# Attention's splits and products with v run on over the ends of head pairs, one unit later, with four tiles of transposed halves

## The chip, the cores and the metric

The kernel runs on one core of a Trainium2 chip. The metric is device time in microseconds (us) of that core for one launch. Before the change the median of three runs is 1622.26 us (1620.82 to 1622.88). The profiled execution was a run of its own, of 1619.84 us.

## The reference, cut to what matters

Two sequences, A and B, of 1024 tokens by 1024 channels go through the same two layers. Weights and inputs are float32. The even layer holds the attention:

```python
def even_layer(x, ...):
    h = rms_norm(x, norm_g)
    pu, pz, q, k, v, az = jnp.split(h @ w_in, EVEN_SPLITS, axis=-1)
    a_out = pool_mixer(pu, pool_w, pool_scale) * silu(pz)
    b_out = axial_gqa(q, k, v, ...) * silu(az)          # 8 query heads of 64, 2 key heads
    return x + concat([a_out, b_out], -1) @ w_out
# in axial_gqa, for each head:
    s = einsum('bqkgd,bskd->bkgqs', q, k) * scale       # 1024 x 1024 scores
    p = softmax(s, axis=-1)
    o = einsum('bkgqs,bskd->bqkgd', p, v)
def odd_layer(x, ...):
    u, vv, z = jnp.split(rms_norm(x) @ w_in, 3, axis=-1)
    sv = w_s (128 x 128 mixing per chunk) applied to rms_norm(gelu(vv)) + b_s
    return x + (gelu(u) * sv * silu(z)) @ w_out
```

## The kernel before, in words

Every float32 operand is cut into two float16 halves (a high part and the rest), and a product is three passes over them. TensorE (PE) does the products, ScalarE (ACT) and VectorE (DVE) cut, scale and take softmax, SyncE (SP) issues all DMAs, the transposing ones among them. Almost all tiles lie in one large SBUF tile, the arena, whose places a planner gives out from the order in which tiles are taken and freed in the Python code.

Attention of one sequence is four head pairs (`attention`, j = 0 to 3). A head pair is 16 units in four groups g: a unit is one tile of 128 queries of one of two heads, and a group is two tiles of two heads. In the texts units are numbered through, S0 to S63 for sequence A and S64 to S127 for B, and a group is written A2.1 (sequence, head pair, group). For a unit, `scores` writes 128 x 1024 scores into one of two PSUM tiles `ps_s` by 4 matmuls (L678), DVE takes the row maximum (L684), ACT the scaled maximum and exp (L685, L686). `split` (ACT L693, DVE L695, ACT L697, DVE L698) normalises and cuts the row into halves, and a transposing DMA (L699) puts them into a tile of the ring `pt`, which has three tiles, one for each group and head. `pv` multiplies a group by v with 48 matmuls (L710), the first half's weights in turn with the second's, one head each, so the first matmul reads head 0's tile and the second head 1's; DVE takes the result out (L714).

In the code, the split of a unit stands after the next unit's scores. The product of group g - 1 stands after the third unit of group g. At the end of a head pair the chain is brought to its end: last split, one portion of filler, last product, then the largest value of the output tile (DVE, L252) and its DMA to DRAM (L734).

Between units, `fill(rate)` puts in other work ("fillers"): the projections of the next head pairs, the pool branch, the other sequence's norms, and for A's rows the output projection (`out_chunks`) while B's attention runs. After A's attention all fillers are drained, `mix_back` brings seven tiles of A's mixed rows back from DRAM (L658), and `split_chunks` cuts the eight tiles into halves (DVE L753 and L756, ACT L755) with a scale over all eight, before the output projection can start.

The order on each engine is not that of the code: a scheduler reorders all instructions by its own model of their times, and each engine then runs its list strictly in that order.

Of the kernel before, what the change touches and what calls it, by code (L numbers as in the profile page):

```python
# [20 lines left out]
P = 128  # L21
# [178 lines left out]
class Kernel:  # L200
    def __init__(self, ctx, tc, args, order, plan):
        self.nc, self.tc, self.order = tc.nc, tc, order
        self.__dict__.update(args)
        self.one = one = ctx.enter_context(tc.tile_pool(name="one", bufs=1))
        self.kept = one.tile([P, 640], F32, name="kept")
        self.kept_at = 0
        self.rings, self.role = {}, "misc"
        self.blocks = {}
        self.arena = Arena(tc.nc, one, plan)
        self.get, self.free = self.arena.get, self.arena.free  # L210
        self.diff = one.tile([P, 2, L], F32R, name="diff")
        self.pw = one.tile([P, 2, 4, P], F32R, name="pw")
        self.ps_s = ctx.enter_context(tc.tile_pool(name="ps_s", bufs=2, space=PSUM))
        self.ps_g = ctx.enter_context(tc.tile_pool(name="ps_g", bufs=3, space=PSUM))
        self.ps_o = ctx.enter_context(tc.tile_pool(name="ps_o", bufs=1, space=PSUM))
        dram = ctx.enter_context(tc.tile_pool(name="dram", bufs=1, space=bass.MemoryType.DRAM))
        self.x1 = [dram.tile([L, D], F32, name=f"x1_{s}") for s in range(2)]
        self.mixed = [dram.tile([8, P, L], F32, name=f"mixed_{s}") for s in range(2)]
        self.w = {"in_e": self.w_in_e, "out_e": self.w_out_e, "in_o": self.w_in_o, "out_o": self.w_out_o}
        self.fillers = deque()  # L220
        self.credit = 0
        self.turned = {}


# [183 lines left out]
    def consts_even(self):  # L408
# [32 lines left out]
        nc.sync.dma_start(out=self.pscale, in_=self.pool_scale.rearrange("(g p) -> p g", p=P))  # L441
        self.edge = self.tiny([P, 4, 2, 8], keep="edge")
        nc.sync.dma_start(out=self.edge, in_=self.edges)
        self.pt = Ring(self, 3, [P, 2, NT, 256], F16)
        self.pf = Ring(self, 3, [P, L], F32)
        self.phl = Ring(self, 4, [P, 2, L], F16)

# [212 lines left out]
    def attention(self, st, j, rate):  # L660
# [28 lines left out]
        def split(tt, h, p, ss):  # L689
            if tt % 2 == 0:  # L690
                pts[tt // 2, h] = self.pt.get()
            s2 = self.tiny([P, 1])
            nc.scalar.activation(out=s2, in_=ss, func=AF.Copy, scale=2.0 ** -15)  # L693
            r = self.tiny([P, 1])
            nc.vector.reciprocal(out=r, in_=s2)  # L695
            hl = self.phl.get()
            nc.scalar.activation(out=hl[:, 0, :], in_=p, func=AF.Copy, scale=r[:, 0:1])  # L697
            nc.vector.scalar_tensor_tensor(out=hl[:, 1, :], in0=p, scalar=r[:, 0:1], in1=hl[:, 0, :], op0=ALU.mult, op1=ALU.subtract)  # L698
            nc.sync.dma_start_transpose(  # L699
                out=pts[tt // 2, h].rearrange("p a t n -> p (a t) n")[:, :, (tt % 2) * P:(tt % 2 + 1) * P],  # L700
                in_=hl.rearrange("p a n -> p (a n)"))
# [11 lines left out]
            cols = slice(g * 256, g * 256 + 256)  # L713
            nc.vector.scalar_tensor_tensor(out=out[:, cols], in0=ps, scalar=sc[:, 0:1], in1=sz[:, cols], op0=ALU.mult, op1=ALU.mult)  # L714

        prev = None
        for g in range(NT // 2):
            for h in range(2):
                for tt in (2 * g, 2 * g + 1):
                    with self.as_role("attention"):  # L720
                        cur = (tt, h) + scores(tt, h)
                        if prev:
                            split(*prev)
                    prev = cur
                    self.fill(rate)
                    if g and h == 1 and tt % 2 == 0:
                        pv(g - 1)
        with self.as_role("attention"):
            split(*prev)
        self.fill(rate)  # L730
        pv(NT // 2 - 1)
        self.amax(st.mam[:, 4 + j:5 + j], out)
        if j < 3:
            nc.sync.dma_start(out=self.mixed[st.s][4 + j], in_=out)  # L734
            self.free(out)
        else:
            st.mix[7] = out
        self.free(sz, st.qT.pop(j))

    def split_chunks(self, tiles, am, keep):  # L740

# [170 lines left out]
    def run(self):  # L912
# [6 lines left out]
        def spread(a, b):  # L919

            out, k = [], 0
            for i, c in enumerate(a):
                out.append(c)
                while k < len(b) and (k + 1) * len(a) <= (i + 1) * len(b):
                    out.append(b[k])
                    k += 1
            return out + b[k:]
# [4 lines left out]
        def pool(st, j):  # L932
            return self.pool_chunks(st, j)
# [31 lines left out]
        for j in range(4):  # L965
            self.attention(A, j, 2950)
        self.drain()
        self.mix_back(A)
        self.free(self.gain_e[0])
        parts_A, split_A = self.split_chunks(A.mix, A.mam, "mixA")  # L970
        self.free(A.kT, A.v)

        def odd_start():
            self.gain_o, self.dh_o = self.gain(self.norm_o, "go", 9)
# [1 line left out]
        nA = self.norm_chunks(A, hA2, self.x1[0], go_, False)  # L976
        vvA = self.vv_chunks(A, True)
        self.fillers.extend(
            spread(qa(B, 1), split_A) + pool(B, 0) + self.out_chunks("out_e", (parts_A, self.xs[0], self.x1[0])) + qa(B, 2) + pool(B, 1)
            + qa(B, 3) + let_go(lambda: [self.rope["q"]]) + [(0, odd_start)] + pool(B, 2) + spread(pool(B, 3), nA[:3]) + let_go(lambda: hB)  # L980
            + spread(vvA[:2], nA[3:]) + vvA[2:11])
        for j in range(4):
            self.attention(B, j, 4250)
        self.drain()
        self.mix_back(B)
        for ring in (self.pt, self.pf, self.phl):
# [100 lines left out]
```

## Time and profile before

| | |
|---|---|
| median of three runs | 1622.26 us |
| profiled execution, its own time | 1619.84 us |
| its span, first to last instruction | 1618.1 us |
| PE busy | 1496.5 us (92%) |
| DVE busy | 1061.8 us (66%) |
| ACT busy | 729.0 us (45%) |
| mean granted TensorE clock | 0.976 |

Attention lies between 78 and about 894 us of the span; A's units to 427 us, B's after it. In that part the matmuls of scores, products and fillers are mixed on PE. A row of the timeline names the engine, the line, what is written and read, and how many instructions are merged, and in brackets how long the engine stood idle before and who released it.

### The profile page before, as it was taken

The page shows a single profiled execution, that of the slowest core. Times are in us where ns is not written, and L with a number is a line of the kernel's source. Part 1 is how long each engine was busy: PE and PEld are TensorE (multiplying, and loading weights), DVE is VectorE, ACT ScalarE, POOL GpSimd, SP SyncE. Part 2 cuts the span into 40 slices and gives each one's busy share as a digit, 9 for nine tenths or more (in the row PEclk, how much of TensorE's full clock was granted, in tenths as well). Part 3 has the DMA queues.
Part 4 walks back from the last instruction along what each step waited for, and adds up shares of the span by engine and source line. Part 5 has one row for each costly group of instructions (what it writes and reads, how often), then busy time and mean ns, then how long its engine had stood idle before and what let it go on. Part 6 is the DMA issues. An engine that isn't in the chain of part 4 may idle for free.

```text
span 1618.1 us, 28061 instructions
## 1 busy us (share of the span) xinstructions
PE 1496.5 (92%) x11751; PEld 1014.1 (63%) x11751; DVE 1061.8 (66%) x1613; ACT 729.0 (45%) x1121; POOL 117.3 (7%) x187
## 2 busy tenths in 40 slices
PE   2989998878799999999799999999999999998999
PEld 1754654557456787464478887554488554467888
DVE  7899999889897675788975854466650643345211
ACT  4367767767664364566755811133432521111000
POOL 2410000102000000000200100010000200000000
PEclk9999999889889999999899999999999999999999
DMA  9558688899948877675997643157210023114121
GB/s 252 116 118 161 150 148 183 186 210 194 213 87 213 211 156 151 144 154 133 224 260 164 186 125 98 40 157 167 81 40 1 27 66 117 46 66 137 60 85 53
DMA packets 497152, 217.69 MB, mean 135 GB/s; under 512 B 366337, under 2 KB 488705, under 8 KB 497025
## 3 DMA queue, kind: packets, MB, share of 16 engines
q1 hardware_dynamic: 497024, 215.90, 57.0%
q8 instruction: 92, 1.51, 0.4%
q14 instruction: 36, 0.29, 0.1%
HBM read 101.04 MB, written 24.12 MB: 77 GB/s over the span
## 4 chain that ended last, share of the span: by engine, by line
PE 57%; DVE 16%; DMA 11%; issue 4%; ACT 4%; POOL 1%; SPq 1%; DVEq 0%; ACTq 0%; POOLq 0%
PE bank L399 35%; PE ps_s L399 17%; DMA arena<-arena 4%; PE bank L710 3%; DVE arena L698 3%; DVE ring_attention L684 3%; PE ps_s L678 3%; DMA arena<-in_w_in_e 2%; DMA arena<-in_w_in_o 1%; DMA arena<-x 1%; ACT arena L686 1%; DVE ring_weights L252 1%; DVE arena L170 1%; DVE arena L756 1%; DVE arena L622 1%
## 5 line engine op out<-in xcount | busy, mean ns | idle before, releaser
L399 PEld LDWEIGHTS <-arena 128*128 128x128 f16 x9600 | 863.9, 99 | 434.1 <-DMA arena<-arena 25.6
L399 PE MATMUL bank<-arena 128*128 128x256 f16 (+2 forms) x8064 | 941.1, 277 | 31.8 <-ACT arena L169 12.7
L399 PE MATMUL ps_s<-arena 128*128 128x512 f16 x1536 | 338.1, 380 | 2.4 <-DVE arena L170 2.4
L169 ACT ACTIVATE arena<-arena,kept 128x1024 f16<-128x1024 f32 x108 | 121.4, 1142 | 281.1 <-DVE kept L281 126.2
L170 DVE SCALAR_TENSOR_TENSOR arena<-arena,kept 128x1024 f16<-128x1024 f32 x108 | 137.6, 1288 | 80.9 <-ACT arena L169 63.9
L698 DVE SCALAR_TENSOR_TENSOR arena<-arena,ring_attention 128x1024 f16<-128x1024 f32 x128 | 163.2, 1278 | 31.3 <-ACT arena L697 29.9
L684 DVE TENSOR_REDUCE ring_attention<-ps_s 128x1 f32<-128x1024 f32 x128 | 155.0, 1216 | 10.8 <-PE ps_s L678 10.5
L697 ACT ACTIVATE arena<-arena,ring_attention 128x1024 f16<-128x1024 f32 x128 | 145.5, 1141 | 36.0 <-DVE ring_attention L695 27.1
L678 PE MATMUL ps_s<-arena 128*128 128x512 f16 x512 | 136.8, 394 | 26.2 <-ACT arena L686 21.5
L686 ACT ACTIVATE arena<-ps_s,ring_attention,kept 128x1024 f32<-128x1024 f32 x128 | 153.7, 1201 | 8.4 <-DVE ring_attention L695 3.7
L784 DVE SCALAR_TENSOR_TENSOR arena<-bank,ring_dout,arena 128x512 f32<-128x512 f32 x64 | 47.9, 749 | 149.7 <-PE bank L399 149.7
L710 PE MATMUL bank<-arena 128*64 128x256 f16 x1536 | 107.7, 290 | 35.7 <-DMA arena<-arena 34.3
L710 PEld LDWEIGHTS <-arena 128*64 128x64 f16 x1536 | 90.2, 117 | 61.2 <-DMA arena<-arena 31.6
L252 DVE TENSOR_REDUCE ring_weights<-arena 128x1 f32<-128x1024 f32 x58 | 70.2, 1215 | 66.6 <-DMA arena<-in_w_in_o 29.4
L678 PEld LDWEIGHTS <-arena 128*128 128x128 f16 x512 | 47.9, 100 | 81.1 <-issue 38.6
L685 ACT ACTIVATE ring_attention<-ring_attention,kept 128x1 f32<-128x1 f32 x128 | 37.1, 290 | 131.4 <-DVE ring_attention L684 131.0
L364 DVE SCALAR_TENSOR_TENSOR arena<-arena,ring_norm 128x1024 f32<-128x1024 f32 x32 | 41.8, 1306 | 25.7 <-POOL ring_norm L318 22.7
L362 ACT ACTIVATE arena<-arena 128x1024 f32<-128x1024 f32 x32 | 33.7, 1054 | 53.1 <-DMA arena<-x 32.9
L903 DVE TENSOR_TENSOR arena<-arena 128x1024 f32<-128x1024 f32 x16 | 19.6, 1223 | 51.2 <-ACT arena L902 51.2
L838 ACT ACTIVATE arena<-bank,ring_dvv 128x256 f32<-128x256 f32 x64 | 26.7, 466 | 54.8 <-PE bank L399 53.9
L902 ACT ACTIVATE arena<-ps_s,ring_duz 128x1024 f32<-128x1024 f32 x16 | 17.7, 1109 | 66.8 <-PE ps_s L399 66.8
L365 ACT CAST arena<-arena 128x1024 f16<-128x1024 f32 x32 | 33.2, 1037 | 23.8 <-DVE arena L364 22.3
(104 smaller groups left out, 883.6 us busy)
## 6 DMA issues: line engine op xcount, KB each, us to landing
arena<-in_w_in_o SPq DMA_DIRECT2D x48, 512.0 KB, 4.4
arena<-in_w_in_e SPq DMA_DIRECT2D x36, 512.0 KB, 4.8
arena<-in_w_out_e SPq DMA_DIRECT2D x16, 512.0 KB, 4.6
x<-arena SPq DMA_DIRECT2D x32, 256.0 KB, 3.0
arena<-x SPq DMA_DIRECT2D x16, 512.0 KB, 4.8
arena<-x SPq DMA_DIRECT2D x32, 256.0 KB, 3.0
out<-arena SPq DMA_DIRECT2D x32, 256.0 KB, 2.1
mixed<-arena SPq DMA_DIRECT2D x14, 512.0 KB, 4.1
```

The costliest lines, as they stand in the source:

```text
L169: nc.scalar.activation(out=hi, in_=raw, func=AF.Copy, scale=s[:, 0:1])
L170: nc.vector.scalar_tensor_tensor(out=lo, in0=raw, scalar=s[:, 0:1], in1=hi, op0=ALU.mult, op1=ALU.subtract)
L252: self.nc.vector.tensor_reduce(out=out, in_=in_, axis=axis, op=ALU.max, apply_absolute_value=True)
L364: nc.vector.scalar_tensor_tensor(out=x, in0=x, scalar=r[:, 0:1], in1=gain[0], op0=ALU.mult, op1=ALU.mult)
L399: self.nc.tensor.matmul(out=o, lhsT=l, rhs=r, start=first and i == 0, stop=last and i == n - 1)
L678: nc.tensor.matmul(out=ps[:, half * 512:half * 512 + 512], lhsT=st.qT[j][:, tt, h, :], rhs=st.kT[:, 4 * half:4 * half + 4, kv, a, :], star ...
L684: nc.vector.tensor_reduce(out=m, in_=ps, axis=AX.X, op=ALU.max)
L686: nc.scalar.activation(out=p, in_=ps, func=AF.Exp, scale=self.s_scale[:, 0:1], bias=nb[:, 0:1], accum_out=ss)
L697: nc.scalar.activation(out=hl[:, 0, :], in_=p, func=AF.Copy, scale=r[:, 0:1])
L698: nc.vector.scalar_tensor_tensor(out=hl[:, 1, :], in0=p, scalar=r[:, 0:1], in1=hl[:, 0, :], op0=ALU.mult, op1=ALU.subtract)
L710: nc.tensor.matmul(out=ps[h * HD:h * HD + HD, :], lhsT=st.v[:, a, t, kv * HD:kv * HD + HD], rhs=pts[g, h][:, b, t, :], start=n < 2, stop=n ...
L784: nc.vector.scalar_tensor_tensor(out=res, in0=ps.rearrange("p (t n) -> p t n", t=2), scalar=box["d"][:, 0:1], in1=res, op0=ALU.mult, op1=A ...
```

## The change

The kernel object now carries the chain from one call to the next. `owed_split` is the split of the unit before, and `owed` a list of products that are due at a unit number. A product of a group is put on the list when its four units are issued, and paid four units later: after the fourth unit of the next group, where it stood after the third. At the end of a head pair nothing is brought to its end: the next pair's scores follow, the last split after the first of them, the last product and the head pair's end (`finish`: largest value, DMA to DRAM, freeing) four units into the next pair. The same holds from A's last head pair into B's first. Only after B's attention does `settle` pay what is left. The ring `pt` has four tiles instead of three, 8 KB more of each partition while attention runs. As A's last tile is finished only during B's first units, `mix_back(A)` is now a filler (`end_A`) behind B's second projections and two portions of pool, and the cutting of A's rows is spread over the rest of that pool portion, where it was spread over the second projections.

```diff
-        self.pt = Ring(self, 3, [P, 2, NT, 256], F16)
+        self.pt = Ring(self, 4, [P, 2, NT, 256], F16)
...
-        prev = None
+        def finish():
+            self.amax(st.mam[:, 4 + j:5 + j], out)
+            if j < 3:
+                nc.sync.dma_start(out=self.mixed[st.s][4 + j], in_=out)
+                self.free(out)
+            else:
+                st.mix[7] = out
+            self.free(sz)
+
         for g in range(NT // 2):
             for h in range(2):
                 for tt in (2 * g, 2 * g + 1):
                     with self.as_role("attention"):
                         cur = (tt, h) + scores(tt, h)
-                        if prev:
-                            split(*prev)
-                    prev = cur
+                        self.owed_split()
+                    self.owed_split = lambda cur=cur: split(*cur)
                     self.fill(rate)
-                    if g and h == 1 and tt % 2 == 0:
-                        pv(g - 1)
+                    self.unit += 1
+                    self.pay(self.unit)
+            self.owed.append((self.unit + 4, lambda g=g: pv(g)))
+        self.owed.append((self.unit + 4, finish))
+        self.free(st.qT.pop(j))
+
+    def pay(self, unit):
+
+        while self.owed and self.owed[0][0] <= unit:
+            self.owed.popleft()[1]()
+
+    def settle(self, rate):
         with self.as_role("attention"):
-            split(*prev)
+            self.owed_split()
+        self.owed_split = lambda: None
         self.fill(rate)
-        pv(NT // 2 - 1)
-        self.amax(st.mam[:, 4 + j:5 + j], out)
...
+        self.pay(self.unit + 4)
...
-        self.mix_back(A)
         self.free(self.gain_e[0])
         parts_A, split_A = self.split_chunks(A.mix, A.mam, "mixA")
-        self.free(A.kT, A.v)
+        qaB, pB0 = qa(B, 1), pool(B, 0)
+
+        def end_A():
+            assert 7 in A.mix
+            self.mix_back(A)
+            self.free(A.kT, A.v)
...
-            spread(qa(B, 1), split_A) + pool(B, 0) + self.out_chunks("out_e", (parts_A, self.xs[0], self.x1[0])) + qa(B, 2) + pool(B, 1)
+            qaB + pB0[:2] + [(0, end_A)] + spread(pB0[2:], split_A) + self.out_chunks("out_e", (parts_A, self.xs[0], self.x1[0])) + qa(B, 2) + pool(B, 1)
...
         for j in range(4):
             self.attention(B, j, 4250)
+        self.settle(4250)
         self.drain()
```

The scheduler makes a new order from this on all engines. On PE it is the same up to S0 and the same again from B's output projection on; between them the same matmuls stand in another order. Lines of the new kernel are one to twelve higher than those of before.

The first place is on DVE where A's attention ends and B's begins. L684 is the row maximum of a unit's scores, L695 and L698 belong to a split, L714 takes a product out of PSUM, and L471 to L479 are the rotation of queries and keys. Before:

```order
L684 TENSOR_REDUCE ring_attention<-ps_s 128x1
L471 TENSOR_TENSOR arena<-arena 128x512
L698 SCALAR_TENSOR_TENSOR arena<-arena,ring_attention 128x1024
L695 RECIPROCAL ring_attention<-ring_attention 128x1
L478 CAST arena<-arena 128x8x64
L698 SCALAR_TENSOR_TENSOR arena<-arena,ring_attention 128x1024
L479 TENSOR_TENSOR arena<-arena 128x8x64
L714 SCALAR_TENSOR_TENSOR arena<-bank,ring_so,arena 128x256
L684 TENSOR_REDUCE ring_attention<-ps_s 128x1
L698 SCALAR_TENSOR_TENSOR arena<-arena,ring_attention 128x1024
L695 RECIPROCAL ring_attention<-ring_attention 128x1
L684 TENSOR_REDUCE ring_attention<-ps_s 128x1
```

And in the changed order, around the same product's L714, now L715 (L685 is the row maximum, L696 and L699 the split, L253 the largest value of the head pair's output):

```order
L699 SCALAR_TENSOR_TENSOR arena<-arena,ring_attention 128x1024
L471 TENSOR_TENSOR arena<-arena 128x4x2x16
L685 TENSOR_REDUCE ring_attention<-ps_s 128x1
L480 TENSOR_TENSOR arena<-arena 128x8x64
L699 SCALAR_TENSOR_TENSOR arena<-arena,ring_attention 128x1024
L685 TENSOR_REDUCE ring_attention<-ps_s 128x1
L170 SCALAR_TENSOR_TENSOR arena<-arena,kept 128x1024
L472 TENSOR_TENSOR arena<-arena 128x512
L715 SCALAR_TENSOR_TENSOR arena<-bank,ring_so,arena 128x256
L696 RECIPROCAL ring_attention<-ring_attention 128x1
L479 CAST arena<-arena 128x8x64
L253 TENSOR_REDUCE kept<-arena 128x1
```

Here the units of B that begin are no longer side by side on DVE: rotation and weights stand between them.

The second place is also on DVE, where A's mixed rows are cut (L753 and L756 before, L765 and L768 now). Before, the maxima of S72 and S73 stand ahead of and behind this whole piece:

```order
L753 TENSOR_SCALAR arena<-arena,kept 128x1024
L698 SCALAR_TENSOR_TENSOR arena<-arena,ring_attention 128x1024
L756 SCALAR_TENSOR_TENSOR arena<-arena,kept 128x1024
L698 SCALAR_TENSOR_TENSOR arena<-arena,ring_attention 128x1024
L756 SCALAR_TENSOR_TENSOR arena<-arena,kept 128x1024 x2
L460 TENSOR_REDUCE ring_rope<-arena 128x8
L753 TENSOR_SCALAR arena<-arena,kept 128x1024
L756 SCALAR_TENSOR_TENSOR arena<-arena,kept 128x1024
L591 SCALAR_TENSOR_TENSOR arena<-arena,bank 128x512
L462 TENSOR_TENSOR arena<-arena,ring_rope 128x512
L464 TENSOR_TENSOR arena<-arena 128x512
L756 SCALAR_TENSOR_TENSOR arena<-arena,kept 128x1024
```

Now the same cutting stands between the maxima of S72, S73 and S74 (L592 and L644 belong to the pool branch, L170 to a weight):

```order
L768 SCALAR_TENSOR_TENSOR arena<-arena,kept 128x1024
L699 SCALAR_TENSOR_TENSOR arena<-arena,ring_attention 128x1024
L592 SCALAR_TENSOR_TENSOR arena<-arena,bank 128x512
L170 SCALAR_TENSOR_TENSOR arena<-arena,kept 128x1024 x2
L685 TENSOR_REDUCE ring_attention<-ps_s 128x1
L768 SCALAR_TENSOR_TENSOR arena<-arena,kept 128x1024
L696 RECIPROCAL ring_attention<-ring_attention 128x1
L765 TENSOR_SCALAR arena<-arena,kept 128x1024
L644 SCALAR_TENSOR_TENSOR arena<-bank,ring_misc,arena 128x512
L592 SCALAR_TENSOR_TENSOR arena<-arena,bank 128x512
L768 SCALAR_TENSOR_TENSOR arena<-arena,kept 128x1024
L685 TENSOR_REDUCE ring_attention<-ps_s 128x1
```

The cutting has moved from a stretch without units into a run of units that follow one another.

## Rows read from the trace of the kernel before

**Rows 1.** The page: busy time by engine; granted clock in 40 slices of the span.

```profile
PE 1496.5 (92%) x11751; PEld 1014.1 (63%) x11751; DVE 1061.8 (66%) x1613; ACT 729.0 (45%) x1121; POOL 117.3 (7%) x187
...
PEclk9999999889889999999899999999999999999999
```

**Rows 2.** Windows, attention's stretches and the rest: busy us and rows by engine.

```profile
78.00:242.00 164.00, 155.34 (x1238) 90.99 (x1235) 153.13 (x279) 111.12 (x188) 12.56 (x17) 0.99 0.71 142
...
340.00:427.00 87.00, 72.76 (x712) 51.69 (x713) 76.93 (x122) 63.76 (x108) 12.42 (x20) 0.92 1.03 210
...
461.00:750.00 289.00, 277.51 (x2355) 190.31 (x2352) 215.18 (x308) 154.40 (x250) 12.36 (x17) 0.99 0.69 156
...
894.00:1618.00 724.00, 710.50 (x5164) 488.65 (x5162) 330.80 (x459) 185.83 (x222) 28.38 (x48) 0.99 0.29 86
```

**Rows 3.** Waits of PE between 78 and 894 us.

```profile
PE bank L710 <- DMA arena<-arena: 34.3, 15, 7.6
PE ps_s L678 <- ACT arena L686: 21.5, 14, 3.0
PE bank L399 <- DMA arena<-arena: 5.6, 5, 2.2
```

**Rows 4.** Windows, four places where units follow closely; columns PE, PEld, DVE, ACT.

```profile
280.00:311.00 31.00, 22.50 (x195) 13.88 (x194) 28.34 (x43) 20.72 (x34) 0.94 (x3) 0.83 0.79 176
339.90:374.80 34.90, 24.85 (x180) 16.26 (x181) 30.58 (x39) 28.98 (x53) 6.61 (x14) 0.85 1.08 222
427.20:455.70 28.50, 16.42 (x109) 8.89 (x107) 24.96 (x35) 20.83 (x39) 1.83 (x2) 0.82 0.94 194
750.50:817.00 66.50, 55.18 (x359) 33.93 (x358) 62.31 (x84) 48.48 (x81) 11.72 (x24) 0.92 0.90 208
```

**Rows 5.** Lines of DVE in attention, mean ns of one.

```profile
L698 DVE SCALAR_TENSOR_TENSOR arena<-arena,ring_attention 128x1024 f16<-128x1024 f32 x128 | 163.2, 1278 | 31.3 <-ACT arena L697 29.9 <-DMA arena<-arena 1.2
L684 DVE TENSOR_REDUCE ring_attention<-ps_s 128x1 f32<-128x1024 f32 x128 | 155.0, 1216 | 10.8 <-PE ps_s L678 10.5
...
L756 DVE SCALAR_TENSOR_TENSOR arena<-arena,kept 128x1024 f16<-128x1024 f32 x32 | 39.2, 1279 | 0.1
```

**Rows 6.** Timeline of PE: matmuls side by side at the full clock.

```profile
72.89 5.34 PE L399 MATMUL bank<-arena 128*128 128x512 f16 x24
78.07 0.59 PE L678 MATMUL ps_s<-arena 128*128 128x512 f16 x2
78.50 2.84 PE L399 MATMUL bank<-arena 128*128 128x128 f16 x48
...
899.31 35.86 PE L399 MATMUL bank<-arena 128*128 128x256 f16 x327
```

**Rows 7.** Timeline of PE: products that wait outside the four places, two with their last scores.

```profile
119.06 2.81 PE L710 MATMUL bank<-arena 128*64 128x256 f16 x47 [2.06 <-DMA arena<-arena]
...
535.95 1.04 PE L678 MATMUL ps_s<-arena 128*128 128x512 f16 x4
...
554.22 4.47 PE L710 MATMUL bank<-arena 128*64 128x256 f16 x47 [3.65 <-DMA arena<-arena]
...
690.65 1.84 PE L710 MATMUL bank<-arena 128*64 128x256 f16 x17 [3.41 <-DMA arena<-arena]
692.42 6.46 PE L399 MATMUL bank<-arena 128*128 128x128 f16 x96
...
867.07 1.04 PE L678 MATMUL ps_s<-arena 128*128 128x512 f16 x4
...
882.34 2.78 PE L710 MATMUL bank<-arena 128*64 128x256 f16 x47 [2.05 <-DMA arena<-arena]
```

**Rows 8.** Timeline of PE: product A3.3 inside the third place.

```profile
435.06 0.42 PE L710 MATMUL bank<-arena 128*64 128x256 f16 x1 [4.64 <-DMA arena<-arena]
...
444.07 5.02 PE L710 MATMUL bank<-arena 128*64 128x256 f16 x47 [1.54 <-DMA arena<-arena]
```

**Rows 9.** DMA issues: KB each, median us from issue to landing.

```profile
arena<-mixed SPq DMA_DIRECT2D x14, 512.0 KB, 5.3
```

More of the change, by code (lines that the diff above doesn't have):

```diff
@@ L221, in __init__ @@
         self.credit = 0
+        self.unit, self.owed, self.owed_split = 0, deque(), lambda: None
         self.turned = {}
@@ L721, in attention @@
                         cur = (tt, h) + scores(tt, h)
-                        if prev:
-                            split(*prev)
-                    prev = cur
+                        self.owed_split()
+                    self.owed_split = lambda cur=cur: split(*cur)
                     self.fill(rate)
-                    if g and h == 1 and tt % 2 == 0:
-                        pv(g - 1)
+                    self.unit += 1
[7 more added lines that the diff above has]
+    def settle(self, rate):
         with self.as_role("attention"):
-            split(*prev)
+            self.owed_split()
+        self.owed_split = lambda: None
         self.fill(rate)
-        pv(NT // 2 - 1)
-        self.amax(st.mam[:, 4 + j:5 + j], out)
[L733 to L738, printed above, removed]
+        self.pay(self.unit + 4)
     def split_chunks(self, tiles, am, keep):
```

## Prediction

> **What bounds the kernel now.** I read the page first. TensorE (PE) is busy for 1496.5 of 1618.1 us and every other engine for far less, so PE is the bound and what can be won is its idle time and its slow stretches; the granted clock falls below nine tenths in a few slices, all of them in attention [rows 1]. The windows come next. Behind 894 us PE is busy for 710.5 of 724 us, and the order on PE there is that of before, so nothing is to be had. Attention, 78 to 894 us, is not of one kind. In its first stretch to 242 us PE and DVE are nearly level (155.3 and 153.1 of 164 us); from 461 to 750 us PE is alone at the limit (277.5 of 289, DVE 215.2) [rows 2]. Then the list of waits: in attention PE waits 34.3 us in all, 15 times, for the transposing DMA of a product (L710), and 21.5 us for the exp that frees a score tile (L678 behind L686) [rows 3]. Where these waits lie decides what the change is worth. I found four places where units follow one another with little filler between, and there PE is busy for only 22.5 of 31, 24.9 of 34.9, 16.4 of 28.5 and 55.2 of 66.5 us at a clock of 0.82 to 0.92, while DVE is busy for 85 to 94% [rows 4]. The third is the end of A's attention. Outside these places stand single waits of products: 2.06 us at 119, 3.65 at 554, 3.41 at 691, 2.05 at 882 us [rows 7].
>
> **A price list for the order.** Side by side at the full clock a 512-column matmul takes 5.18 / 24 = 0.216 us and a 128-column one about 2.84 / 48 less the last one's drain, 0.056; a 256-column one 35.86 / 327 = 0.11, say 0.108; a product's matmul 2.71 / 47 = 0.058 from the start at 882.34 to the filler behind it [rows 6, 7]; for a pool matmul I take an estimate of 0.25, as it is a little dearer than a 512-column one. On DVE the row maximum takes 1.216, the second half of a split 1.278, that of A's mixed rows 1.279 us [rows 5]; the shorter ones I took from the same view. With these I add up what stands between two units in the order on PE and on DVE. As a test, before: the four places are S40 to S44, S48 to S56, S64 to S72 and S112 to S120. Their DVE sums are 27.7, 33.0, 29.3 and 69.4 us, 159.4 in all, and their lengths 31, 34.9, 28.5 and 66.5 us, 160.9 in all [rows 4]. So there DVE's list sets the time, to 1%, and the products' waits in them (4.64 and 1.54 us for A3.3 [rows 8], among others) are only how PE spends it. Their PE sums are 18.3, 20.4, 11.1 and 49.3, together 99.1 us: the places cost 61.8 us over PE's work.
>
> **The change part by part.**
> *The four places.* The change takes the third one apart: from S64 to S72 PE now has 38 us of work, kept busy by filler that earlier ran only behind it. But the filler that is used up there is missing later, and the cutting of A's rows, which stood in a stretch of filler, now stands between units. The new close run is S72 to S82. On DVE it has ten maxima (12.2 us), eight splits (10.2), seven second halves of mixed rows (9.0) and three first halves (2.2), four maxima of other tiles (4.9), two weights (2.6), and some 6.4 us of smaller work: 47.5 us; on PE 27.6. So 19.9 us are lost there where 28.5 - 11.1 = 17.4 were lost at the boundary. The others: S40 to S44 now 17.1 on DVE against 7.5 on PE, S48 to S56 35.7 against 26.1, S112 to S127, where the close run now lies at the end, 83.9 against 63.3. Together 184.2 - 124.5 = 59.7 us, against 61.8: a gain of 2.1, which is within the error of such sums. I take nothing for it.
> *The products outside.* Between a group's last scores and the product's second matmul the order on PE held 19.0 us of work for A0.0, 13.7 for B0.3, 14.2 for B2.0 and 12.6 for B3.3. The way from scores to landing took 18.3 us for B0.3 (535.95 to 554.22) and 15.3 for B3.3 (867.07 to 882.34) [rows 7], so these came too early. Now the distances are 25.2, 27.8, 24.9 and 34.6 us: all four waits go, 2.06 + 3.65 + 3.41 + 2.05 = 11.2 us. What would be late next, the filler behind, has no wait in these rows. With the two longer ones goes a slow clock: 47 matmuls in 4.47 instead of 2.78 us, 17 in 1.84 instead of 1.0 and 96 in 6.46 instead of 96 x 0.056 = 5.4 us [rows 7], 3.6 us in all.
> *New short distances.* A0.1 and A0.2 now have 17.6 and 18.9 us (20.0 and 21.9 before), and the first matmul of A1.3 follows its second unit by 17 where it was 21. The nearest row is A0.0, which with 19.0 waited 2.06. I take 3 us for the three, with 0 and 3 x 2.06 = 6 as ends. And S64 to S72, now filled, has 44 us by the sums on DVE against 38 on PE. The first stretch, equally mixed, shows both engines level and PE at 95% [rows 2], so I take 1 us and keep 0 and 6 as ends.
> *Tail of a head pair.* The maximum of an output (1.2 us on DVE) and its DMA on SP's queue come four units later, none is added; behind the maximum wait only splits, and the DMA is read by `mix_back` alone. The seven loads of A's mixed rows take 5.3 us each from issue to landing [rows 9]; they now stand in SP's list behind 56 to 66 transposes instead of 55 to 63, some ten units ahead of the last cutting, so that cover hides them. If it is gone, the output projection's first portion waits for one load, up to 5.3 us.
> *A fourth tile of the ring.* It takes 8 KB from the arena, whose plan changes everywhere. A weight's load that must wait for its place is seen in attention only as PE's wait for a DMA at a filler, 5.6 us in five waits [rows 3]. From minus 5.6 to plus 5.6 then; I take 0. On the other side the ring was never what a product waited for in the rows above, so the tile by itself gives nothing but the room for the later products.
> *Sum.* -11.2 - 3.6 + 3 + 1 = -10.8, say -11 us, against the profiled execution's 1619.84 us: 1609. The median of the runs is 2.4 us higher than that execution, so I forecast 1611.
>
> **A rule against a row.** From 340 to 427 us the 16 DMA engines have a busy share of 1.03 at 210 GB/s [rows 2], which reads as if the transposes there could not land sooner whatever the order. The Trainium skill (DMA: Bandwidth & Descriptors, "Latency and other measured facts") gives 261 GB/s for a transposing DMA, so by that page there would be a fifth of room. By the row the products of A3 gain nothing from a later place; by the page their waits could go too, which is the first rival. No run here shows the page's figure.
>
> **The rivals.**
> 1. *The waits in the close places go as well.* The way of a unit gets shorter because SP's queue and the transposes have room, and PE runs through these places with less loss than DVE's list says. For it: 34.3 us of waits for transposes in all [rows 3], of which 34.3 - 11.2 = 23 lie inside. Against it: DVE's sums alone make up the lengths of these places. If half goes: -11 - 11.5, so 1600 us.
> 2. *No change.* The scheduler puts products where its model sees them ready, so a later place in the code need not be a later place in the list. For it: A2.1, with the longest single wait of all, has 13.9 us where it had 13.7, and the close places cost 59.7 instead of 61.8. It decides if the new short distances eat what the four waits give: 1622.
> 3. *Slower: short products that wait on top of DVE.* In the new close places five products come early: A2.1 at 13.9, B0.1 at 15.1, B0.2 at 10.6, B3.1 at 13.7 and B3.2 at 12.3 us behind their last scores, and the way takes 15 to 18. If each holds PE, and with it the next scores that DVE needs, as A3.3 did (4.64 + 1.54 us [rows 8]), DVE idles and that comes on top of its list: up to 5 x 6.2 = 31 us, with half of it +15.5. It decides from 11 us on. Against it: A3.3 and B0.0 did just that at the old boundary, and that place was no longer than its list. At two thirds, +20: 1631 us.
>
> **How the numbers follow.** The forecast of 1611 gets 0.50, with an own range of 1603 to 1619 from the ends of the short distances and of the arena's plan. Rival 1 gets 0.16, rival 2 0.14 and rival 3 0.20. What this kernel's measurement can tell from no change is about 0.2%, 3.2 us. Faster than that are nearly all of the first (0.47), and rival 1: 0.63. Within 0.2% are rival 2 and the first one's upper edge: 0.17. Slower: 0.20. The range runs from 1596, below rival 1, to 1629, just short of rival 3's middle.
>
> **What would show it.** Right: no wait of a product at A0.0, B0.3, B2.0 and B3.3; PE busy at the end of A's attention with a clock near 1; a new stretch of some 48 us with PE at about 28 us of work around S72 to S82, DVE full in it, and another at the end of B's attention; behind it the same 724 us. Wrong would be: the stretch S72 to S82 much shorter than DVE's list (rival 1) or much longer, with products waiting in it for transposes (rival 3); a wait of the output projection for `mixed`; or PE's idle time in attention grown at fillers that wait for weights.

## The result and the profile after

The changed kernel takes 1633.43 us (median of 5 runs, 1631.79 to 1636.63), the kernel before beside it 1622.88 (5 runs, 1620.82 to 1625.8). The ratio is 1.0069, with a 95% interval of 1.0054 to 1.0085: slower by some 11 us, where 1611 was forecast.

The profiled execution has a span of 1631.6 us, 13.5 more than before. Its page, busy time of PE and the granted clock in 40 slices:

```profile
PE 1502.2 (92%) x11751; PEld 1014.8 (62%) x11751; DVE 1056.7 (65%) x1613; ACT 726.5 (45%) x1121; POOL 115.7 (7%) x187
...
PEclk9999999899998999999889999999999999998999
```

Against [rows 1] PE is busy for 5.7 us longer with the same 11751 matmuls (the mean granted clock is 0.969 where it was 0.976), and 13.5 - 5.7 = 7.8 us longer idle. So two shares, idle time and slow matmuls, and the list of PE's waits names the first. From 78 to 905 us (engine, line, what released it: us in total, times, longest):

```profile
PE ps_s L679 <- ACT arena L687: 32.2, 13, 7.9
PE bank L711 <- DMA arena<-arena: 19.4, 9, 4.8
PE ps_s L679 <- DMA arena<-arena: 10.6, 3, 6.3
PE bank L400 <- DMA arena<-arena: 9.0, 4, 5.8
PE bank L291 <- DVE diag L271: 5.3, 2, 4.3
PE bank L400 <- ACT arena L169: 2.5, 2, 1.3
```

The products' waits for transposes fell from 34.3 to 19.4 us [rows 3], as meant. But scores waiting for the exp of two units before rose from 21.5 to 32.2, scores waiting for transposed queries or keys from 4.7 to 10.6, fillers waiting for a DMA from 5.6 to 9.0, waits for the scale of a weight (L290, now L291) from 1.3 to 5.3, and those for its cast by ACT (L169) are new. Summed over all rows of that list PE waits for 77.2 us before and 83.5 after.

The windows of the places where units now follow closely, S40 to S44, S48 to S56, S72 to S82 and S112 to S127, with S64 to S72 as the third row, and the stretch behind attention (columns PE, PEld, DVE, ACT, POOL, then clock, DMA share, GB/s):

```profile
282.00:300.60 18.60, 10.31 (x69) 5.73 (x68) 18.60 (x25) 14.92 (x27) 0.93 (x3) 0.72 0.63 131
336.60:383.10 46.50, 33.55 (x233) 22.57 (x234) 35.65 (x40) 33.93 (x58) 7.48 (x14) 0.85 0.96 211
...
440.90:482.90 42.00, 41.69 (x265) 21.99 (x266) 36.88 (x65) 27.94 (x48) 4.26 (x5) 0.93 0.87 185
482.90:526.90 44.00, 31.97 (x223) 18.41 (x222) 43.95 (x57) 30.19 (x50) 0.00 (x0) 0.88 0.70 166
742.00:829.70 87.70, 71.42 (x450) 39.61 (x449) 79.88 (x108) 61.41 (x104) 10.85 (x21) 0.90 0.82 180
...
904.90:1631.60 726.70, 711.92 (x5166) 490.49 (x5163) 330.51 (x459) 185.62 (x222) 24.54 (x48) 0.99 0.29 85
```

In S40 to S44 and S72 to S82 DVE is busy all the time. In S112 to S127 it is idle for 7.8 us, and in S48 to S56 it is busy for only 35.65 of 46.5 us, so there something else holds. S64 to S72 is filled now, PE is busy for 41.69 of 42 us. PE's timeline shows what holds in S48 to S56, and the other new waits (start, us, line, what, and in brackets the idle time before):

```profile
372.63 5.30 PE L400 MATMUL bank<-arena 128*128 128x256 f16 x24 [5.83 <-DMA arena<-arena]
...
440.94 3.60 PE L679 MATMUL ps_s<-arena 128*128 128x512 f16 x8 [6.31 <-DMA arena<-arena]
...
506.37 1.86 PE L679 MATMUL ps_s<-arena 128*128 128x512 f16 x4 [4.79 <-ACT arena L687]
...
523.16 2.78 PE L711 MATMUL bank<-arena 128*64 128x256 f16 x47 [2.83 <-DMA arena<-arena]
...
556.64 0.29 PE L291 MATMUL bank<-diag,ones 128*128 128x128 bf16 x1 [4.28 <-DVE diag L271]
...
796.09 1.86 PE L679 MATMUL ps_s<-arena 128*128 128x512 f16 x4 [7.94 <-ACT arena L687]
...
858.48 0.27 PE L711 MATMUL bank<-arena 128*64 128x256 f16 x1 [3.96 <-DMA arena<-arena]
...
1196.67 0.22 PE L291 MATMUL bank<-diag,ones 128*128 128x128 bf16 x1 [4.38 <-DVE diag L271]
```

At 372.63 a filler (keys and values of B) waits for B's transposed norm, at 440.94 B's first scores for transposed queries or keys, at 556.64 and, far behind attention, at 1196.67 a weight's scale is late. At 858.48 the last product waits although its last scores began 29 us earlier. SP's queue shows why (issue, us, line; L700 transposes a unit, L368 a norm, L153 loads a weight):

```profile
843.76 5.63 SPq L368 DMA_TRANSPOSE arena<-arena  x2
849.49 1.11 SPq L153 DMA_DIRECT2D arena<-in_w_in_o  x2
850.69 9.79 SPq L700 DMA_TRANSPOSE arena<-arena  x3
```

The last three units' transposes stand behind those of a norm and behind weight loads.

Both traces can be laid side by side by the work that PE had done (each matmul at its price at the full clock). The changed kernel is 3.6 us ahead at 274 us of before's span, 6.8 behind at 374, 9.5 ahead at 505 (A's end now is filled: it wins 16.3 us there), 4.3 behind at 530, 6.1 ahead at 791, 11.1 behind at 889 and 13.5 at the end. So it loses 10 us around S48 to S56, wins 16 at the boundary, gives 14 of these back at S72 to S82, and loses 17 us at the end of B.

### The profile page after: what moved, and what is told of

It reads as the page before. It is cut to its first block, busy times and chain, and to the rows that moved or that the text cites. A ratio compares the mean times of both kernels' runs of the same rounds, so it can differ in the third digit from the quotient of the medians.

```text
span 1631.6 us, 28051 instructions
## 1 busy us (share of the span) xinstructions
PE 1502.2 (92%) x11751; PEld 1014.8 (62%) x11751; DVE 1056.7 (65%) x1613; ACT 726.5 (45%) x1121; POOL 115.7 (7%) x187
## 5 line engine op out<-in xcount | busy, mean ns | idle before, releaser
L169 ACT ACTIVATE arena<-arena,kept 128x1024 f16<-128x1024 f32 x108 | 121.6, 1143 | 310.0 <-DVE kept L282 110.8
L170 DVE SCALAR_TENSOR_TENSOR arena<-arena,kept 128x1024 f16<-128x1024 f32 x108 | 137.4, 1285 | 101.2 <-ACT arena L169 87.1
L679 PE MATMUL ps_s<-arena 128*128 128x512 f16 x512 | 139.2, 399 | 43.0 <-ACT arena L687 32.2
L699 DVE SCALAR_TENSOR_TENSOR arena<-arena,ring_attention 128x1024 f16<-128x1024 f32 x128 | 163.0, 1276 | 20.8 <-ACT arena L698 19.8
L698 ACT ACTIVATE arena<-arena,ring_attention 128x1024 f16<-128x1024 f32 x128 | 145.1, 1141 | 42.7 <-DVE ring_attention L696 33.4
L685 DVE TENSOR_REDUCE ring_attention<-ps_s 128x1 f32<-128x1024 f32 x128 | 154.6, 1213 | 8.2 <-PE ps_s L679 8.1
L253 DVE TENSOR_REDUCE ring_weights<-arena 128x1 f32<-128x1024 f32 x58 | 70.4, 1214 | 81.3 <-DMA arena<-in_w_in_o 54.8
L711 PE MATMUL bank<-arena 128*64 128x256 f16 x1536 | 101.9, 280 | 19.5 <-DMA arena<-arena 19.4
L711 PEld LDWEIGHTS <-arena 128*64 128x64 f16 x1536 | 85.0, 112 | 45.3 <-issue 27.5
L365 DVE SCALAR_TENSOR_TENSOR arena<-arena,ring_norm 128x1024 f32<-128x1024 f32 x32 | 41.0, 1280 | 25.2 <-POOL ring_norm L319 25.1
L316 POOL TENSOR_SCALAR ring_norm<-ring_norm 128x1 f32<-128x1 f32 x32 | 13.6, 424 | 459.5 <-ACT arena L363 342.0
L896 DVE SCALAR_TENSOR_TENSOR arena<-bank,kept,arena 128x512 f32<-128x512 f32 x32 | 22.9, 747 | 35.7 <-PE bank L400 35.5
```

Source lines behind the costliest of these rows:

```text
L169: nc.scalar.activation(out=hi, in_=raw, func=AF.Copy, scale=s[:, 0:1])
L170: nc.vector.scalar_tensor_tensor(out=lo, in0=raw, scalar=s[:, 0:1], in1=hi, op0=ALU.mult, op1=ALU.subtract)
L253: self.nc.vector.tensor_reduce(out=out, in_=in_, axis=axis, op=ALU.max, apply_absolute_value=True)
L365: nc.vector.scalar_tensor_tensor(out=x, in0=x, scalar=r[:, 0:1], in1=gain[0], op0=ALU.mult, op1=ALU.mult)
L679: nc.tensor.matmul(out=ps[:, half * 512:half * 512 + 512], lhsT=st.qT[j][:, tt, h, :], rhs=st.kT[:, 4 * half:4 * half + 4, kv, a, :], star ...
L685: nc.vector.tensor_reduce(out=m, in_=ps, axis=AX.X, op=ALU.max)
```

## The experiments

A kernel's plan of places and the scheduler's order are made anew from every edit. Ratios are to the kernel before on the same chip, with 95% intervals.

**Where is the loss?** Three theories: it lies at B's end, which runs bare (end theory), at B's first units (boundary theory), or in the 8 KB of the fourth tile (memory theory).

*The fourth tile alone.*

```diff
-        self.pt = Ring(self, 3, [P, 2, NT, 256], F16)
+        self.pt = Ring(self, 4, [P, 2, NT, 256], F16)
```

> The kernel before, with only the fourth tile in the ring (products, head-pair ends and the boundary as before). End theory (what the change loses, it loses where B's last units run bare of filler, because running on over a head pair's end leaves out that end's portion of filler): the fourth tile alone is worth nothing, 1622 us (1618 to 1627), product waits as before. Boundary theory (the cutting of A's rows between B's first units is the loss): the same, 1622. Memory theory (8 KB less for the weights' places makes loads late and PE waits for them, in the tail too): 1628 to 1636, with a wait of some 4 us for a weight's scale in the tail as after the change.

1632.2 us, ratio 1.0067 (1.0053 to 1.008): as much as the whole change, in the memory theory's range. It differs from the kernel before in one thing more, as all runs made from the changed kernel do: a head pair's queries are freed one split earlier in the code, and that, too, goes into the plan. Its waits on PE:

```profile
PE ps_s L679 <- ACT arena L687: 31.2, 17, 5.9
PE bank L711 <- DMA arena<-arena: 26.3, 18, 3.8
```

The scores' waits are up as in the changed kernel, with no product moved in the code. The memory theory's sign, a scale some 4 us late in the tail, is not there as named: L291 has no wait behind 905 us, and one of 2.59 us stands behind L293 at 993.43.

*Every head pair ended, only A's last runs on into B.*

```diff
         for j in range(4):
             self.attention(A, j, 2950)
+            if j < 3:
+                self.settle(2950)
...
             self.attention(B, j, 4250)
-        self.settle(4250)
+            self.settle(4250)
```

> The changed kernel, but every head pair is brought to its end as before, except that A's last one runs on into B's first (fourth tile and product one unit later kept). In the order on PE 144 us of work stand between B's last scores and B's output projection, where the kernel before has 141 and the changed one 180. End theory: the 17 us that the changed kernel loses from 785 to 889 us come back, 1615 to 1620 us, faster than before. Boundary theory: the loss stays, 1630 to 1635. Memory theory: 1630 to 1636.

1643.85 us, 1.014 (1.0127 to 1.0154). The end theory's 1615 to 1620 is missed by far, the others' ranges by 8.

*A ended before B starts, head pairs run on inside.* `self.settle(2950)` stands behind A's loop, and `mix_back(A)` and the cutting stand where they stood before.

> The changed kernel, but A's attention is brought to its end before B's starts, and A's rows are brought back and cut as before (head pairs run on over their ends inside a sequence, fourth tile and product one unit later kept). 167 us of PE work stand behind B's last scores. End theory: about two thirds of the loss at B's end stay and the gain at the boundary is not there, 1626 to 1632 us. Boundary theory: 1615 to 1620, since the close run at S72 to S82 is gone. Memory theory: 1630 to 1636.

1622.53 us, 1.0007 (0.9998 to 1.0017): no range holds it.

*More filler per unit in B.* `self.attention(B, j, 4700)` for 4250.

> The changed kernel with one number changed: 4700 instead of 4250 ns of filler per unit during B's attention, so that the filler used between B's units is 4.7 x 65 = 306 us instead of 4.25 x 65 = 276 (before: 4.25 x 68 = 289). 132 us of PE work stand behind B's last scores instead of 180. End theory: B's last 8 units are no longer bare and some 10 of the 17 us lost there come back, 1619 to 1626 us; what S112 to S120 has less of filler keeps the rest. Boundary theory and memory theory: nothing is changed at their places, 1630 to 1636.

1637.63 us, 1.0099 (1.0085 to 1.0113). The end theory's range is missed by 12, the others' by 1.6. S120 to S127 have filler again, but the loss moved ahead of them: S112 to S120 now take 51.6 us with 34.32 of them busy on PE, where the changed kernel took 45.1 us, nearly all busy:

```profile
769.60:821.20 51.60, 34.32 (x220) 20.11 (x218) 49.44 (x64) 35.88 (x60) 7.56 (x15) 0.80 0.92 215
```

**Memory, or the draw of an order?**

*8 KB held empty beside three tiles, in the kernel before.*

```diff
+        self.pad = self.get([P, 2048], F32, long=True)
         self.pf = Ring(self, 3, [P, L], F32)
```

> The kernel before with the ring of three tiles, and 8 KB of the arena held beside it for as long as the ring lives, which nothing writes or reads. Memory theory (the fourth tile is paid for by 8 KB that other tiles no longer have, so loads for the other sequence's norm are listed later and fillers that hang on them come late): as with the fourth tile alone, 1628 to 1635 us, with the first load of the second norm in B's attention behind 700 us instead of 674. Ring theory (four tiles let the splits and transposes bunch): 1620 to 1625. Scatter theory (any new plan of the arena gives another order and costs up to 10 us more or less): no forecast.

1645.58 us, 1.0145 (1.0121 to 1.0169), worse than the tile itself and above every range:

```profile
PE ps_s L679 <- ACT arena L687: 29.0, 15, 6.8
...
PE ps_s L679 <- DMA arena<-arena: 10.9, 3, 6.8
PE bank L290 <- DVE diag L270: 8.9, 4, 4.1
```

The three kinds of waits that the change brought are all here, with the order of the code untouched. The memory theory's sign came too: the first load of the second norm (L358) is issued at 724.61 us where it was at 674.11. But a late load alone costs nothing that shows: it stands at 734.47 us in the kernel before with SLACK 0.030 below, which is the faster one.

*The planner's number alone.* `SLACK = 0.040` for 0.035 in the kernel before. The planner prefers places that will have lain free for longer, up to this share of the whole.

> The kernel before with one number of the arena's planner changed (SLACK 0.040 instead of 0.035): no memory is taken and no code moves, but places and so the order of the scheduler are new. Memory theory and ring theory: 1619 to 1626 us. Scatter theory: off by 5 us or more, either way.

1630.61 us, 1.0055 (1.0037 to 1.0072): a new plan without any edit is worth 8 us, as only the scatter theory had it. Its scores, too, wait longer for exp, and 7.6 us are lost before attention begins:

```profile
PE ps_s L678 <- ACT arena L686: 32.2, 14, 5.7
PE bank L710 <- DMA arena<-arena: 18.6, 14, 2.7
```

*Run on inside a sequence, with three tiles and the product where it was.* `Ring(self, 3, ...)`, and `self.unit + 3` for both entries of `owed`, with A ended before B.

> Head pairs run on over their ends inside a sequence, but with three tiles and the product after the third unit of the next group; A is brought to its end before B starts, as before. Memory theory: what this loses to the same with four tiles and a later product (1622.5 us) is the memory, so 1612 to 1617 us, faster than before. Ring theory: 1612 to 1620. Scatter theory: 1622 to 1632, as the other new orders.

1625.76 us, 1.0019 (1.0007 to 1.0031): in the scatter theory's range alone.

*Run on everywhere, with three tiles and the product where it was.*

```diff
-        self.pt = Ring(self, 4, [P, 2, NT, 256], F16)
+        self.pt = Ring(self, 3, [P, 2, NT, 256], F16)
...
-            self.owed.append((self.unit + 4, lambda g=g: pv(g)))
-        self.owed.append((self.unit + 4, finish))
+            self.owed.append((self.unit + 3, lambda g=g: pv(g)))
+        self.owed.append((self.unit + 3, finish))
```

> The changed kernel with three tiles and the product after the third unit of the next group: the chain runs on over head pairs and from A into B, and A's rows come back as in the changed kernel. Memory theory: the 11 us that the fourth tile cost alone come back, 1620 to 1625 us. Ring theory: the same. Scatter theory: 1622 to 1640.

1610.56 us, 0.9935 (0.9914 to 0.9956): faster than both kernels and below every range.

```profile
PE bank L400 <- DMA arena<-arena: 19.0, 5, 6.4
PE ps_s L679 <- ACT arena L687: 17.1, 10, 4.2
PE bank L711 <- DMA arena<-arena: 13.5, 8, 3.3
```

The scores' and the products' waits are low here, while fillers wait longer for a DMA than in any other of these kernels. Is that the version or its draw?

**The same versions under three plans.**

*Four tiles in that version* (`Ring(self, 4, ...)`, product still after the third unit).

> The version that ran at 1610.6 us (the chain runs on over all ends, product after the third unit, three tiles), now with four tiles and nothing else. Memory theory (a fourth tile costs what other tiles lose of the arena, about 11 us, as it did on the kernel before): 1619 to 1626 us. Scatter theory (every new plan of places gives a new order, and orders differ by some 10 us whatever was changed; 1610.6 was a good draw and so was the kernel before): 1612 to 1635 with no rule, most likely near 1625. Later-product theory (the loss of the change lies in the product one unit later): 1608 to 1614, as with three tiles.

1623.67 us, 1.001 (0.9995 to 1.0024): 13 us above the same with three tiles. The later-product theory's range is missed, the other two hold it.

*The changed kernel with SLACK 0.040.*

> The changed kernel with the planner's SLACK at 0.040 instead of 0.035, as in the unchanged kernel's run at 1630.6 us. Memory theory: 1630 to 1640, some 10 us or more above the three-tile version with the same number. Scatter theory: 1615 to 1640, and its distance to the three-tile version is as likely to be of either sign.

1641.05 us, 1.0115 (1.0091 to 1.014): 1 us above both ranges.

*The three-tile version with SLACK 0.040.*

> The three-tile version that ran at 1610.6 us with SLACK 0.040. Memory theory: 1608 to 1620 us, below the changed kernel and below the kernel before with the same number (1630.6). Scatter theory: 1620 to 1635, the good draw is gone.

1619.83 us, 0.9988 (0.9978 to 0.9998): in the memory theory's range, just below the other.

*The kernel before with SLACK 0.030.*

> The kernel before with SLACK 0.030: a second new plan of places with nothing else changed. Scatter theory: 1625 to 1635 like that with 0.040 (the number in use was a good draw), or at least 4 us away from 1622. Memory theory: 1619 to 1626.

1618.75 us, 0.9978 (0.9967 to 0.9989): just outside both.

*The three-tile version with SLACK 0.030.*

> The run-on version with three tiles and the product after the third unit, with SLACK 0.030. Ladder theory (the parts add up, whatever the plan: run-on -11.5, fourth tile +12, product one unit later +10): 1618.75 - 11.5 = 1607 us, 1602 to 1613. Scatter theory: within 7 us of 1622 on either side, 1615 to 1629.

1637.28 us, 1.0081 (1.0063 to 1.0099). The ladder theory fell, and the scatter theory's range is missed by 8 as well. Its scores wait as little as in the good draw, but the products wait longer than before the change:

```profile
PE bank L711 <- DMA arena<-arena: 37.5, 16, 8.0
...
PE ps_s L679 <- ACT arena L687: 17.0, 10, 3.8
```

*With four tiles.*

> The same with four tiles. Ladder theory: 1619 us, 1613 to 1625, and 8 us or more above the run with three. Scatter theory: 1615 to 1629, and either may be the faster one.

1625.31 us, 1.0016 (1.0007 to 1.0026), below the run with three, in the scatter theory's range.

*The changed kernel with SLACK 0.030.*

> The changed kernel (four tiles, product one unit later) with SLACK 0.030. Ladder theory: 1629 us, 1623 to 1636, the slowest of the three. Scatter theory: 1615 to 1629, in no order with the others.

1635.52 us, 1.0076 (1.0061 to 1.0091): in the ladder theory's range but not the slowest of the three; 6 above the scatter theory's.

*The three-tile version at 0.035, with 8 KB held empty as above.*

> The run-on version with three tiles that ran at 1610.6 us, with 8 KB of the arena held empty beside the ring while it lives. Memory theory (the fourth tile costs through the place it takes): 1620 to 1633 us. Tile theory (what costs is that four tiles let units run ahead of filler): 1607 to 1615.

1624.99 us, 1.0013 (1.0003 to 1.0022): 14 us above the same without them. The memory theory's range holds, the tile theory fell.

*The product one unit later, every end as before, four tiles.* The edit of the ended head pairs above, for A's last one too, with `self.unit + 4`.

> The kernel before with four tiles and the product one unit later, every head pair and A itself brought to its end as before. The same without the later product ran at 1632.2 us. Later-product theory (the later place by itself costs about 10 us): 1637 to 1647. Scatter theory: 1624 to 1640, above or below 1632 with equal chance.

1657.27 us, 1.0219 (1.0197 to 1.0241), the slowest of all, 10 above one range and 17 above the other.

*The changed kernel at SLACK 0.040 with `self.unit + 3`.*

> The changed kernel under SLACK 0.040 (1641.1 us) with the product after the third unit of the next group again. Later-product theory: 1626 to 1636. Scatter theory: anything from 1618 to 1645, above or below 1641 by no rule.

1649.15 us, 1.0173 (1.0151 to 1.0195), above the 1641 with the later product: the later-product theory fell, and the scatter theory's range is missed by 4.

```profile
PE ps_s L679 <- ACT arena L687: 40.4, 16, 8.8
PE bank L711 <- DMA arena<-arena: 30.1, 17, 6.2
```

The medians side by side, in us (the kernel before at 0.035 is the 1622.26 of its first three runs):

| SLACK | before | run on, 3 tiles | run on, 4 tiles | changed kernel |
|---|---|---|---|---|
| 0.030 | 1618.8 | 1637.3 | 1625.3 | 1635.5 |
| 0.035 | 1622.3 | 1610.6 | 1623.7 | 1633.4 |
| 0.040 | 1630.6 | 1619.8 | 1649.2 | 1641.1 |
| mean | 1623.9 | 1622.6 | 1632.7 | 1636.7 |

Within a column the times scatter with a standard deviation of 10.5 us (pooled over the four), so the difference of two means of three has an error of 10.5 x sqrt(2/3) = 8.6. The changed kernel is above the kernel before in each row, by 16.8, 11.2 and 10.4 us. The steps between the columns are -1, +10 and +4; none is as much as twice its error.

Six pairs at 0.035 stand outside the table's steps. By the same medians a tile more, or 8 KB held empty, costs 9.9 and 23.3 us on the kernel before and 14.4 on the run-on version; the later product costs 25.1 on the kernel with ended head pairs; running on gains 8.5 there with four tiles, and 23.8 with the later product as well. With these the means of all pairs are some +13 us for the 8 KB (five of six pairs up), +9 for the later product (three of four up) and -7 for running on (four of five down), and one pair has an error of 10.5 x sqrt(2) = 15.

All twenty orders give one thing more, by a division made after the runs. The seven with the whole arena have a mean of 1623.6 us, the thirteen with 8 KB less (by the tile or held empty) 1636.3: 12.7 more, with an error of 10.5 x sqrt(1/7 + 1/13) = 4.9. Seven of the thirteen also have the later product; the six without it have 1633.5, 9.9 more than the seven, with an error of 5.8. Between the groups of seven and of thirteen the mean of the scores' waits for exp goes from 21.1 to 29.6 us, that of waits for a scale or a cast, which are mostly a weight's, from 2.3 to 6.8, and PE's busy time from 1497.6 to 1503.6 us. The products' waits for transposes fall from 27.9 to 23.3 us, and those of fillers for a DMA from 13.4 to 10.2.

## Why the prediction was wrong

*The products' waits.* Right in the main. A0.0, B0.3 and B2.0 start without a wait, as does B3.3's second matmul; its first has a new one, 3.96 us at 858.48. So the 11.2 us that were counted went and 3.96 came back; over all products the waits fell from 34.3 to 19.4 us. The new short distances (A0.1, A0.2, A1.3) wait for nothing: 0 where 3 were taken. The 3.6 us that were to come from a faster clock did not show in the total: by the page the products' matmuls are busy for 101.9 us where they were for 107.7, but those of scores and fillers for longer, and PE in all for 5.7 us more.

*The four close places.* Here the first step failed: "So there DVE's list sets the time", and with it the term "I take nothing for it". The places took 196.8 us where 184.2 were counted, so over PE's work they cost 196.8 - 124.5 = 72.3 us, where 61.8 had been and 59.7 were forecast. These 12.6 us are half of the 24 between the sum's -11 and the measured +13.5. S40 to S44, S72 to S82 and S112 to S127 came out near their sums: 18.6, 44.0 and 87.7 us where 17.1, 47.5 and 83.9 were counted. S48 to S56 took 46.5 where 35.7 were, and DVE was idle there for 10.9 of them: the filler that should stand between the units waited for transposes, with the 16 DMA engines busy at 0.96. That the rule passed its test before, to 1%, was luck. By [rows 4] DVE was busy for only 146.2 of the 160.9 us there (88 to 94% in each place), while the prices counted too much, as one DVE instruction begins some 0.08 us before the one ahead of it ends (1.22 us from 428.60 on, the next at 429.74, in the trace of before):

```profile
428.60 1.22 DVE L684 TENSOR_REDUCE ring_attention<-ps_s 128x1 f32<-128x1024 f32 x1
429.74 1.27 DVE L698 SCALAR_TENSOR_TENSOR arena<-arena,ring_attention 128x1024 f16<-128x1024 f32 x1
```

The two errors were of like size and hid each other.

*The fourth tile.* The second step that failed: "From minus 5.6 to plus 5.6 then; I take 0." The tile alone on the kernel before cost some 11 us and 8 KB held empty some 23, each in one plan, and the orders with 8 KB less have a mean 12.7 us higher. The bounds came from one row, fillers that wait for a DMA [rows 3], but that row is lower in the orders with 8 KB less (10.2 us where the others have 13.4), and what is higher there is scores that wait for exp, weights' scales, and PE's busy time. How the 8 KB would do this is not shown: no row tells why a load stands where it stands in SP's list.

*What no step had.* The sum treats every wait that it does not name as unchanged. But a new plan gives a new order, and that alone moved the unchanged code by -3.5 and +8.4 us. A term "a new draw, plus or minus 10" was missing, and without it a range of 8 us on either side was too narrow. The kernel before was no lucky draw by its own three plans: 1618.8, 1622.3 and 1630.6 us.

*Rival 3* gave about the right time, 1631 us, by half of its mechanism, and so by luck. Its five products waited, A2.1 for 4.81 and 1.65 us, B0.2 for 2.83, B3.1 for 1.74, B3.2 for 1.43 and B0.1 for nothing, 12.5 us of the 31 that it allowed. But the closed places became longer than their DVE list mainly at S48 to S56, where no such product stands. *Rival 1* is out: the close places grew, where by it they shrink. The rule of the Trainium skill that was weighed beside it (DMA: Bandwidth & Descriptors, "Latency and other measured facts") stays open: S48 to S56, full of transposes, moved 211 GB/s at a share of 0.96, where [rows 4] had 222, and neither shows the 261 which that page gives for a non-contiguous middle dimension. *Rival 2* is out as well: the short distances ate nothing.

*The tail* was not "the same 724": it takes 726.7 us. A weight's scale comes 4.38 us late at 1196.67, on a matmul that did not move in PE's order. DVE's list there and the loads behind it are new as well, and which of them made it late is not shown.

*Sums in the prediction.* The 23 us of waits "inside" the close places hold 1.25 us at 250 us and 0.37 at 663 that lie outside. And the ends that its sum names add up to 1601 to 1625 us, not to 1603 to 1619; the measured time is outside of both.

*What stays open*: how the 11 us divide, and why the filler at S48 to S56 came late. The transpose that it waits for at 372.63 was issued at 366.71 and had its halves from DVE at 364.6; why these stand so far behind in DVE's list no row tells. The changed kernel was slower than the kernel before under each of three plans, so the loss is not the draw of one plan alone. By the means the 8 KB and the later product cost about as much (+13 and +9 over all pairs, +10 and +4 in the table), and running on gains some or nothing; but single pairs go from -12 to +29 us for the tile, from -8 to +25 for the later product and from -24 to +19 for running on.

## What to carry to other kernels

Where a planner and a scheduler make the order, an edit is also a new draw: rebuild both versions under two or three harmless settings before a difference of 1% is put down to the edit. A buffer added to an arena that is nearly full is not free because its own use is off the path; hold the same bytes empty to see what they cost. A sum of prices that matches a length proves no limit: the row of the same window says whether that engine was busy all the time. And a wait counted as removed is only won if what comes next on that engine is ready, so ask for each engine which list ends last in the new order, transposes and weight loads among them.

## What the runs showed of the hardware

A transposing DMA of a unit holds SP for some 3 us in these rows (9.79 us for three at 850.69). While a norm's and the units' transposes overlap, from 300 to 343 us of the changed kernel, SP's list has no gap over 2 us, and ready units queue behind it: the halves of S47 are done on DVE at 325.91 us and their transpose is issued at 335.93, 10 us later. Whether SP is held up by the 16 DMA engines these rows don't tell. And idle time went together with slow matmuls: over the twenty kernels, the group with 13.5 us more of span has 7.6 us of these as idle time of PE and 6.0 in PE's busy time, with the same matmuls.
